# Weight-stationary projections: the high weights move over high and low activations in one 512-column matmul

## The chip, the cores and the metric

The kernel runs on one core of a Trainium2 chip. The metric is the device time of one execution in microseconds (us), the median of several runs; a shorter time is better. The engines of the core run side by side and wait for one another through semaphores: TensorE (PE for its matmuls, PEld for its loads of stationary operands), VectorE (DVE), ScalarE (ACT), GpSimd (POOL) and SyncE (SP), whose queue issues the weight transfers.

## The reference

Two layers, each of three sub-layers with an RMSNorm before and after, on 256 tokens of 1024 features, in float32. Layer 0 mixes tokens by a gated short convolution, layer 1 by a gated DeltaNet (GDN).

```python
def swiglu(x, w_gate_up, w_down):
    gate, up = jnp.split(x @ w_gate_up, 2, axis=-1)
    return (jax.nn.silu(gate) * up) @ w_down

def short_conv_mixer(x, w_in, conv_w, w_out):
    b, c, v = jnp.split(x @ w_in, 3, axis=-1)
    y = b * causal_depthwise_conv(c * v, conv_w)
    return y @ w_out
...
    for i in range(DEPTH):
        g = norm_g[i]
        ff = swiglu(rms_norm(h, g[0]), ffn_w_gate_up[i, 0], ffn_w_down[i, 0])
        h = h + 0.5 * rms_norm(ff, g[1])
        m_in = rms_norm(h, g[2])
...
        h = h + rms_norm(mix, g[3])
        ff = swiglu(rms_norm(h, g[4]), ffn_w_gate_up[i, 1], ffn_w_down[i, 1])
        h = h + 0.5 * rms_norm(ff, g[5])
```

The four FFNs have 2816 hidden features each, so a gate-and-up weight is 1024 x 5632 and a down weight 2816 x 1024.

## The kernel before, in words

Every float32 factor is split into a high and a low part of a faster matmul type (float32r). A product is then the sum of three: high by high, high activations by low weights, low activations by high weights.

**Weights.** A unit is 512 KB of weights, 128 partitions x 1024. `unit` (L102) loads it into one of 3 `raw` buffers by the SP queue, ACT writes its high part `whi` (L111), DVE the low part `wlo` = raw - `whi` (L113). There are 8 pairs of `whi` and `wlo` buffers. A slab of an input projection is four units: 1024 input rows (8 steps k of 128) by 512 output columns. So two slabs fit on the chip.

**Activations.** After the pre-norm, `pre_norm` (L160) transposes a token tile of 128 tokens on PE and writes the high and low part of the transposed activations, `xh` and `xl`, each 128 partitions x 2 token tiles x 8 k x 128 tokens.

**Input projections.** The first slabs of a sub-layer (two; one in the first) go one token tile after the other, with the activations stationary and 512 weight columns moving (`act_group`, L203, lines L214, L215, L218). All later slabs go by `stat_group` (L237): 128 weight columns are stationary, the 256 tokens of both tiles move, and per k there are three matmuls of 256 columns, L245 (`whi`, `xh`), L246 (`whi`, `xl`) and L247 (`wlo`, `xh`), each with its own load of the stationary operand. All 24 matmuls of a group add into one 256-column half of a PSUM bank. A slab of an FFN has four groups: gate and up of two blocks j of 128 hidden features. The pool `ps` has four banks (tile name `mm`), `ps_acc` the other four.

**Reading the groups.** In an FFN, per j: ACT takes silu of the gate half from PSUM (L335, `sg`), DVE multiplies it by the up half from PSUM (L337, `hf`), ACT and DVE write its high and low part (L338, L339; `hh`/`hl` or parts of `hb`). In the short convolution, ACT copies one half (L386) and DVE multiplies (L387); in its last two slabs DVE multiplies the gate `y` by a whole bank of two groups (L405). In the GDN a short convolution reads the groups directly (L517, L519).

**Output projections.** `out_proj` (L251) goes in chunks of one unit, the activations stationary, 512 weight columns moving (L263, L264, L265), with token tile 1 six chunks behind tile 0.

**Order.** The program is written as one stream of PE work; the framework's scheduler places every instruction in the queue of its engine, and each engine works through its queue in that order. Chains of the GDN are resumed by ticks between groups. All DMAs of weights are issued by SP as `raw` buffers come free.

Of the kernel before, what the change touches and what calls it, by code (L numbers as in the profile page):

```python
# [24 lines left out]
LAG = 6  # chunks by which token tile 1 follows tile 0 in an output projection  # L25
SPLIT = 1024  # columns per hi/lo split instruction
HEAD = 2  # slabs whose token tiles are projected one after the other at the start of a sub-layer
HEAD0 = 1  # the same for the first sub-layer
NW = 8  # hi/lo weight units on chip
NRAW = 3  # raw weight units on chip  # L30
NSMALL = 22  # 2 KB slots
NBIG = 8  # 4 KB slots
NROW = 3  # [128, 1024] work rows
KQ_WAIT = 3  # waits of the side chains, in ticks
# [3 lines left out]
ORD = "00111222"  # which mark of the norm chain each head unit is split after  # L38
GORD = "00012222"  # the same in the GDN
GSPLIT = 1024  # SPLIT of the GDN head  # L40
TPOS = 1  # output projection steps left when the next input is transposed
DEFER = 4  # k steps by which the low part of the activations lags
DEFER0 = 0  # the same in the first sub-layer
# [3 lines left out]
GUACT = 1  # decay operands built on ScalarE  # L47
# [3 lines left out]
def trunk_kernel(ctx: ExitStack, tc: tile.TileContext, x, norm_g, w_gu, w_dn, sc_in, sc_cw, sc_out,  # L51
# [144 lines left out]

    def new_xT():
        xh = sp.tile([P, NT, KD, P], F32R, name="xh", bufs=1)
        xl = sp.tile([P, NT, KD, P], F32R, name="xl", bufs=1)
        return xh, xl  # L200

# [1 line left out]
    def act_group(pt, w, t, xh, xl, defer=0):  # L203
        """Activations of token tile t stationary; all columns of the slab move."""
        per = KD // len(w)
        width = w[0][0].shape[-1] // per
        def part(k):
            c = slice((k % per) * width, (k % per + 1) * width)
            return w[k // per][0][:, c], w[k // per][1][:, c]

        for k in range(KD + defer):
            if k < KD:
                hi, lo = part(k)
                PE.matmul(pt, lhsT=xh[:, t, k, :], rhs=hi, start=(k == 0), stop=False)  # L214
                PE.matmul(pt, lhsT=xh[:, t, k, :], rhs=lo, start=False, stop=False)  # L215
            if k >= defer:
                j = k - defer
                PE.matmul(pt, lhsT=xl[:, t, j, :], rhs=part(j)[0], start=False, stop=(j == KD - 1))  # L218
                if j % 2:
                    tk.tick()  # L220

    def head_slabs(ws, xh, xl, evac, mid, defer=DEFER):
        """The first slabs, one token tile after the other (weights of all of them stay)."""
        late = None
        for t in range(NT):
            if t == 1:
                mid()
            for i, w in enumerate(ws):
                n = w[0][0].shape[-1] * len(w) // KD
                pt = ps.tile([P, n], F32, name="mm")  # L230
                act_group(pt, w, t, xh, xl, 0 if i else defer)
                if late is not None:
                    late()
                late = evac(t, i, pt)
        return late

    def stat_group(ptile, w, col, xh, xl):  # L237
        """Weights of 128 columns stationary; both token tiles move."""
# [11 lines left out]

    def out_proj(srcs, yh, yl, finish, last, lag=LAG):  # L251
        """yh/yl(c, t) -> [128 ch, 128 tok] operands; accumulates token-major [128, 1024]."""
# [39 lines left out]
    def ffn_proj(layer, ab, xh, xl, mid, head=HEAD):  # L292
# [31 lines left out]
        for s in range(head, NSLAB):  # L324
            alloc(s)
            w = load_slab(src[s])
            for j in range(2):
                pt = ps.tile([P, 512], F32, name="mm")
                stat_group(pt[:, 0:256], w, j * P, xh, xl)
                stat_group(pt[:, 256:512], w, 256 + j * P, xh, xl)  # L330
                if late is not None:
                    late()
                    late = None
                sg = sp.tile([P, 256], F32, name="sg")
                S.activation(sg, pt[:, 0:256], AF.Silu)  # L335
                hf = sp.tile([P, 256], F32, name="hf")
                V.tensor_tensor(hf, sg, pt[:, 256:512], ALU.mult)  # L337
                S.activation(hh[s][:, j, :], hf, AF.Copy)  # L338
                V.tensor_tensor(hl[s][:, j, :], hf, hh[s][:, j, :], ALU.subtract)  # L339
# [5 lines left out]
    def sc_proj(xh, xl, mid):  # L345
# [32 lines left out]
        for s in range(4):  # L378
            if s >= HEAD:
                w = load_slab(sc_in[s])  # L380
                for j in range(2):
                    pt = ps.tile([P, 512], F32, name="mm")
                    stat_group(pt[:, 0:256], w, j * P, xh, xl)
                    stat_group(pt[:, 256:512], w, 256 + j * P, xh, xl)
                    sg = sp.tile([P, 256], F32, name="sg")
                    S.activation(sg, pt[:, 0:256], AF.Copy)  # L386
                    V.tensor_tensor(cv[s][:, j, :], sg, pt[:, 256:512], ALU.mult)  # L387
# [6 lines left out]
        for s in range(2):  # L394
            w = load_slab(sc_in[4 + s])
            for i in range(2):
# [4 lines left out]
                pt = ps.tile([P, 2, T], F32, name="mm")  # L401
                for j in range(2):
                    stat_group(pt[:, j, :], w, (2 * i + j) * P, xh, xl)
                hf = sp.tile([P, 2, T], F32, name="yb")
                V.tensor_tensor(hf, y[2 * s + i], pt, ALU.mult)  # L405
# [4 lines left out]
    def gdn_proj(xh, xl, mid):  # L410
# [14 lines left out]
        # -- beta, log decay and their exponentials, both token tiles at once --  # L425
# [15 lines left out]
        def gates():  # L441
# [10 lines left out]
            # log1p(e) = 2 atanh(z), z = e / (2 + e) <= 1/3, by its series in z^2  # L452
# [55 lines left out]
        # -- keys and queries, channel-major: short conv, silu --  # L508
# [29 lines left out]
        def kq_chain():  # L538
            """Per pair of key heads: norms, scaled decayed k k^T and k q^T, diagonal blocks."""
# [56 lines left out]
        # -- unit lower triangular inverse: 32x32 blocks one per lane, then 64x64 on the tensor engine --  # L596
# [53 lines left out]
        # -- values: conv, silu, token-major, scaled by |k| --  # L650
# [18 lines left out]
        # -- delta rule of four value heads over the two token tiles --  # L669
# [87 lines left out]
        # -- gate, norm weight, channel-major operands of the output projection --  # L757
# [29 lines left out]
        # -- order of work: head columns [b a | k0 q0 k1], [q1 k2 q2 k3], then q3, k4, q4, ... --  # L787
# [106 lines left out]
def layout(x, norm_g, ffn_w_gate_up, ffn_w_down, sc_w_in, sc_conv_w, sc_w_out,  # L894
# [3 lines left out]
    def slabs(w, groups, width):  # L898
        """(1024, groups*n*width) -> [n, 4, 128, 2*groups*width]."""
# [5 lines left out]
    def cols(parts, n):  # L905
        """(1024, width) -> [n, 128, 8 / n * width]."""
        w = np.concatenate(parts, axis=1)
        return c(w.reshape(n, KD // n, P, w.shape[1]).transpose(0, 2, 1, 3).reshape(n, P, -1))
# [51 lines left out]
```

## Time and profile before

| What | Value |
|---|---|
| Time, median of 3 runs | 1155.92 us (1155.24 to 1156.04) |
| Span of the profiled execution | 1153.1 us |
| What the median has beyond that span | 2.8 us |
| PE busy | 1119.9 us (97%), 7584 matmul records |
| PEld busy | 1013.7 us (88%) |
| DVE busy | 691.3 us (60%) |
| ACT busy | 600.8 us (52%) |
| Groups L245, L246, L247 | 1512 matmuls each |
| Mean granted TensorE clock | 0.995 |

The profile is of one execution, which has a span from its first to its last instruction and no other time of its own. A matmul record lasts from issue to the modelled end of its drain, so records overlap and a busy PE says little; the distance from one start to the next (the pitch) tells what a matmul takes of the stream. A granted clock of 1.0 is 2.4 GHz, of 0.5 is 1.2 GHz.

### The profile page before, as it was taken

How to read it: one execution, taken by the hardware profiler on the slowest of the kernel's cores; microseconds unless marked ns; L12 is line 12 of the kernel's file. 1: busy time of each engine (PE TensorE's matmuls, PEld its weight loads, DVE VectorE, ACT ScalarE, POOL GpSimd, SP SyncE). 2: the span in 40 equal slices, each digit the busy share in tenths (PEclk: the TensorE clock that was granted, in tenths of full speed). 3: DMA queues.
4: the chain of work that ended last, by engine and by line, in shares of the span. 5: the costliest groups of instructions: out<-in, count | busy, mean ns of one | idle time of the engine just before them, and what ended most of it. 6: DMA issues, size and time to landing. Idle time of an engine off the chain costs nothing.

```text
span 1153.1 us, 18985 instructions
## 1 busy us (share of the span) xinstructions
PE 1119.9 (97%) x7584; PEld 1013.7 (88%) x7584; DVE 691.3 (60%) x981; ACT 600.8 (52%) x1027; POOL 80.3 (7%) x145
## 2 busy tenths in 40 slices
PE   6999999999999999999999999888999999999997
PEld 5999987899799998789998887877998877999986
DVE  5665535785765553565554478778865567655443
ACT  5654534544554443555443368875676546545432
POOL 1000000000200000010000012210310212000000
PEclk9999999999999999999999999999899999999999
DMA  7755555665576455566555653246424145655552
GB/s 260 225 195 198 167 177 177 216 198 171 183 219 201 165 198 167 166 218 202 194 172 167 195 173 110 92 134 195 147 92 156 47 135 167 219 193 171 194 164 74
DMA packets 55959, 198.78 MB, mean 172 GB/s; under 512 B 6720, under 2 KB 7232, under 8 KB 55872
## 3 DMA queue, kind: packets, MB, share of 16 engines
q1 hardware_dynamic: 55872, 197.58, 52.9%
q8 instruction: 59, 0.97, 0.3%
q14 instruction: 28, 0.23, 0.1%
HBM read 196.51 MB, written 1.05 MB: 171 GB/s over the span
## 4 chain that ended last, share of the span: by engine, by line
PE 79%; DVE 7%; ACT 6%; DMA 4%; issue 2%; POOL 2%; SPq 0%; DVEq 0%; POOLq 0%; ACTq 0%
PE mm L245 15%; PE mm L247 15%; PE mm L246 15%; PE acc L263 7%; PE acc L264 7%; PE acc L265 7%; PE mm L214 3%; PE mm L215 3%; PE mm L218 3%; DVE wlo L113 2%; DMA raw<-in_w_gu 2%; ACT whi L111 2%; ACT blk L585 1%; ACT junk L145 1%; DVE kq L519 1%
## 5 line engine op out<-in xcount | busy, mean ns | idle before, releaser
L113 DVE TENSOR_TENSOR wlo<-raw,whi 128x1024 fp32r<-128x1024 f32 (+2 forms) x362 | 436.4, 1218 | 338.1 <-ACT whi L111 336.6
L111 ACT ACTIVATE whi<-raw 128x1024 fp32r<-128x1024 f32 (+2 forms) x362 | 373.2, 1052 | 362.2 <-PE acc L265 103.7
L245 PE MATMUL mm<-xh,whi 128*128 128x256 f32 x1512 | 432.1, 286 | 2.0 <-DVE kq L519 2.0
L246 PE MATMUL mm<-xl,whi 128*128 128x256 f32 x1512 | 430.3, 285 | 0.0
L247 PE MATMUL mm<-xh,wlo 128*128 128x256 f32 x1512 | 429.9, 284 | 0.1
L245 PEld LDWEIGHTS mm<-xh,whi 128*128 128x128 f32 x1512 | 291.4, 193 | 3.1 <-DVE kq L519 2.4
L246 PEld LDWEIGHTS mm<-xl,whi 128*128 128x128 f32 x1512 | 291.7, 193 | 0.5 <-issue 0.2
L247 PEld LDWEIGHTS mm<-xh,wlo 128*128 128x128 f32 x1512 | 291.5, 193 | 0.7 <-DVE wlo L113 0.3
L263 PE MATMUL acc<-whi,hb 128*128 128x512 f32 x352 | 137.1, 389 | 0.0
L264 PE MATMUL acc<-wlo,hb 128*128 128x512 f32 x352 | 135.8, 386 | 0.2 <-DVE wlo L113 0.2
L265 PE MATMUL acc<-whi,hb 128*128 128x512 f32 x352 | 135.7, 386 | 0.0
L215 PE MATMUL mm<-wlo,xh 128*128 128x512 f32 (+1 forms) x240 | 95.1, 396 | 1.5 <-DVE wlo L113 1.4
L214 PE MATMUL mm<-whi,xh 128*128 128x512 f32 (+1 forms) x240 | 95.5, 399 | 0.8 <-ACT xh L173 0.6
L218 PE MATMUL mm<-whi,xl 128*128 128x512 f32 (+1 forms) x240 | 88.7, 392 | 0.0
L263 PEld LDWEIGHTS acc<-whi,hb 128*128 128x128 f32 x352 | 66.2, 188 | 14.1 <-issue 1.2
L264 PEld LDWEIGHTS acc<-wlo,hb 128*128 128x128 f32 x352 | 66.2, 188 | 13.5 <-DVE wlo L113 0.5
L265 PEld LDWEIGHTS acc<-whi,hb 128*128 128x128 f32 x352 | 66.1, 188 | 13.3
L151 POOL TENSOR_SCALAR rstd<-ss 128x1 f32<-128x1 f32 x24 | 12.2, 509 | 825.9 <-ACT junk L145 825.9
L215 PEld LDWEIGHTS mm<-wlo,xh 128*128 128x128 f32 x240 | 45.7, 190 | 12.6 <-DVE wlo L113 4.4
L214 PEld LDWEIGHTS mm<-whi,xh 128*128 128x128 f32 x240 | 45.7, 191 | 11.4 <-ACT xh L173 2.3
L218 PEld LDWEIGHTS mm<-whi,xl 128*128 128x128 f32 x240 | 45.6, 190 | 9.2 <-DVE xl L174 0.4
L335 ACT ACTIVATE sg<-mm 128x256 f32<-128x256 f32 x74 | 27.5, 372 | 33.8 <-PE mm L247 33.8
(202 smaller groups left out, 976.1 us busy)
## 6 DMA issues: line engine op xcount, KB each, us to landing
raw<-in_w_gu SPq DMA_DIRECT2D x176, 512.0 KB, 4.3
raw<-in_w_dn SPq DMA_DIRECT2D x88, 512.0 KB, 3.7
raw<-in_sc_in SPq DMA_DIRECT2D x24, 512.0 KB, 4.2
raw<-in_gdn_z SPq DMA_DIRECT2D x16, 512.0 KB, 3.8
raw<-in_gdn_v SPq DMA_DIRECT2D x16, 512.0 KB, 4.2
raw<-in_gdn_out SPq DMA_DIRECT2D x16, 512.0 KB, 3.3
gamma<-in_norm_g SPq DMA_DIRECT2D x12, 512.0 KB, 5.8
raw<-in_gdn_a SPq DMA_DIRECT2D x9, 512.0 KB, 4.2
```

The lines of the kernel that those rows point to most:

```text
L111: S.activation(hi[:, r], raw[:, r], AF.Copy)
L113: V.tensor_tensor(lo[:, r], raw[:, r], hi[:, r], ALU.subtract)
L214: PE.matmul(pt, lhsT=xh[:, t, k, :], rhs=hi, start=(k == 0), stop=False)
L215: PE.matmul(pt, lhsT=xh[:, t, k, :], rhs=lo, start=False, stop=False)
L218: PE.matmul(pt, lhsT=xl[:, t, j, :], rhs=part(j)[0], start=False, stop=(j == KD - 1))
L245: PE.matmul(ptile, lhsT=hi, rhs=xh[:, :, k, :], start=(k == 0), stop=False)
L246: PE.matmul(ptile, lhsT=hi, rhs=xl[:, :, k, :], start=False, stop=False)
L247: PE.matmul(ptile, lhsT=lo, rhs=xh[:, :, k, :], start=False, stop=(k == KD - 1))
L263: PE.matmul(o, lhsT=yh(c, t), rhs=hi[:, r], start=(c == 0), stop=False)
L264: PE.matmul(o, lhsT=yh(c, t), rhs=lo[:, r], start=False, stop=False)
L265: i = PE.matmul(o, lhsT=yl(c, t), rhs=hi[:, r], start=False, stop=(c == n - 1)).ins
L335: S.activation(sg, pt[:, 0:256], AF.Silu)
```

## The change

`xh` and `xl` become the two halves of one tile `x2`. A new `wide_group` takes the place of `stat_group` in the FFNs and in the short convolution (the GDN keeps `stat_group`). Per k it makes one matmul of 512 columns, `whi` stationary, over the 256 high and the 256 low activation columns, into both halves of a PSUM bank, and one of 256 columns, `wlo` by the high activations, into the second half. The first half then holds high by high, the second the two corrections. `total` reads a group: ACT copies the second half to `corr`, DVE adds the first half from PSUM to it. A group now fills a bank of its own, and silu and the products read the sums in SBUF. Comments are taken out as well, and line numbers move: L264 and L265 are the wide and the narrow matmul, L273 and L274 the copy and the add.

```diff
     def new_xT():
-        xh = sp.tile([P, NT, KD, P], F32R, name="xh", bufs=1)
-        xl = sp.tile([P, NT, KD, P], F32R, name="xl", bufs=1)
-        return xh, xl
...
+        x2 = sp.tile([P, 2, NT, KD, P], F32R, name="x2", bufs=1)
+        both.append(x2)
+        return x2[:, 0], x2[:, 1]
...
+    def wide_group(w, col):
...
+        pt = ps.tile([P, 2, T], F32, name="mm")
+        xx = both[-1]
...
+            PE.matmul(pt, lhsT=hi, rhs=xx[:, :, :, k, :], start=(k == 0), stop=False)
+            PE.matmul(pt[:, 1, :], lhsT=lo, rhs=xx[:, 0, :, k, :], start=False, stop=(k == KD - 1))
...
+    def total(pt, dst):
...
+        c = sp.tile([P, T], F32, name="corr")
+        S.activation(c, pt[:, 1, :], AF.Copy)
+        V.tensor_tensor(dst, pt[:, 0, :], c, ALU.add)
...
-                pt = ps.tile([P, 512], F32, name="mm")
-                stat_group(pt[:, 0:256], w, j * P, xh, xl)
-                stat_group(pt[:, 256:512], w, 256 + j * P, xh, xl)
+                pg = wide_group(w, j * P)
+                pu = wide_group(w, 256 + j * P)
...
-                sg = sp.tile([P, 256], F32, name="sg")
-                S.activation(sg, pt[:, 0:256], AF.Silu)
-                hf = sp.tile([P, 256], F32, name="hf")
-                V.tensor_tensor(hf, sg, pt[:, 256:512], ALU.mult)
+                sg = sp.tile([P, T], F32, name="sg")
+                total(pg, sg)
+                S.activation(sg, sg, AF.Silu)
+                hf = sp.tile([P, T], F32, name="hf")
+                total(pu, hf)
+                V.tensor_tensor(hf, sg, hf, ALU.mult)
...
-                    stat_group(pt[:, j, :], w, (2 * i + j) * P, xh, xl)
-                hf = sp.tile([P, 2, T], F32, name="yb")
-                V.tensor_tensor(hf, y[2 * s + i], pt, ALU.mult)
+                    total(wide_group(w, (2 * i + j) * P), hf[:, j, :])
+                V.tensor_tensor(hf, y[2 * s + i], hf, ALU.mult)
```

PE's queue inside a weight-stationary stream of the first FFN, before:

```order
L245 MATMUL mm<-xh,whi 128x256
L246 MATMUL mm<-xl,whi 128x256
L247 MATMUL mm<-xh,wlo 128x256
L245 MATMUL mm<-xh,whi 128x256
L246 MATMUL mm<-xl,whi 128x256
L247 MATMUL mm<-xh,wlo 128x256
```

and of the changed kernel (`x_90` is the tile `x2`):

```order
L264 MATMUL mm<-x_90,whi 128x512
L265 MATMUL mm<-x_90,wlo 128x256
L264 MATMUL mm<-x_90,whi 128x512
L265 MATMUL mm<-x_90,wlo 128x256
L264 MATMUL mm<-x_90,whi 128x512
L265 MATMUL mm<-x_90,wlo 128x256
```

Three matmuls and three loads of a k step have become two of each; the moving columns of a step are 768 in both.

DVE's queue over one slab in the middle of the first FFN, before:

```order
L113 TENSOR_TENSOR wlo<-raw,whi 128x1024 x2
L337 TENSOR_TENSOR hf<-sg,mm 128x256
L113 TENSOR_TENSOR wlo<-raw,whi 128x1024
L339 TENSOR_TENSOR hb<-hf,hb 128x256
L113 TENSOR_TENSOR wlo<-raw,whi 128x1024
L337 TENSOR_TENSOR hf<-sg,mm 128x256
L339 TENSOR_TENSOR hb<-hf,hb 128x256
```

and one slab there in the changed kernel:

```order
L113 TENSOR_TENSOR wlo<-raw,whi 128x1024 x2
L274 TENSOR_TENSOR hf<-mm,corr 128x256
L113 TENSOR_TENSOR wlo<-raw,whi 128x1024
L363 TENSOR_TENSOR hf<-sg,hf 128x256
L274 TENSOR_TENSOR sg<-mm,corr 128x256
L365 TENSOR_TENSOR hb<-hf,hb 128x256
L113 TENSOR_TENSOR wlo<-raw,whi 128x1024
L274 TENSOR_TENSOR hf<-mm,corr 128x256
L363 TENSOR_TENSOR hf<-sg,hf 128x256
L365 TENSOR_TENSOR hb<-hf,hb 128x256
L274 TENSOR_TENSOR sg<-mm,corr 128x256
```

Four adds L274, one per group, have come between the four splits L113 of the next units.

ACT's queue over one slab of the same FFN, before:

```order
L111 ACTIVATE whi<-raw 128x1024
L335 ACTIVATE sg<-mm 128x256
L338 ACTIVATE hb<-hf 128x256
L111 ACTIVATE whi<-raw 128x1024 x3
L335 ACTIVATE sg<-mm 128x256
L338 ACTIVATE hb<-hf 128x256
```

and in the changed kernel:

```order
L273 ACTIVATE corr<-mm 128x256
L111 ACTIVATE whi<-raw 128x1024
L360 ACTIVATE sg<-sg 128x256
L111 ACTIVATE whi<-raw 128x1024
L273 ACTIVATE corr<-mm 128x256
L111 ACTIVATE whi<-raw 128x1024
L273 ACTIVATE corr<-mm 128x256
L364 ACTIVATE hb<-hf 128x256
L111 ACTIVATE whi<-raw 128x1024
L360 ACTIVATE sg<-sg 128x256
L273 ACTIVATE corr<-mm 128x256
L364 ACTIVATE hb<-hf 128x256
```

Four copies L273 have come in, each waiting for the end of its group on PE, and the four `whi` splits of a slab stand between them.

## Rows read from the trace of the kernel before

**Rows 1.** The page's first part (busy time and share of the span by engine, instructions) and, from the view of the cores, the span and the mean granted clock.

```profile
PE 1119.9 (97%) x7584; PEld 1013.7 (88%) x7584; DVE 691.3 (60%) x981; ACT 600.8 (52%) x1027; POOL 80.3 (7%) x145
core 0: 1153.1 us, clock 0.995
```

**Rows 2.** Everything that PE waited for in the whole span, longest in total first: who waited for whom, us in total, times, longest us.

```profile
PE mm L171 <- DVE xs L164: 12.3, 6, 8.9
PE mm L662 <- ACT yb L506: 3.7, 1, 3.7
PE acc L551 <- ACT kq L506: 2.1, 1, 2.1
PE mm L245 <- DVE kq L519: 2.0, 1, 2.0
PE acc L554 <- DVE KQ L578: 1.7, 1, 1.7
PE mm L215 <- DVE wlo L113: 1.4, 2, 1.2
PE acc L637 <- ACT blk L630: 0.7, 1, 0.7
PE acc L467 <- DVE glog L463: 0.6, 1, 0.6
PE mm L214 <- ACT xh L173: 0.6, 1, 0.6
PE acc L551 <- ACT junk L563: 0.6, 2, 0.4
PE acc L264 <- DVE wlo L113: 0.2, 1, 0.2
PE acc L626 <- DVE blk L613: 0.2, 1, 0.2
```

**Rows 3.** Five stretches that lie inside the weight-stationary streams of the first FFN, the short convolution and the other three FFNs: the stretch in us, its length, busy us (and instructions) of PE, PEld, DVE, ACT and POOL, granted clock, share of the DMA engines, GB/s.

```profile
30.00:142.00 112.00, 112.00 (x934) 111.94 (x933) 63.68 (x81) 59.25 (x85) 0.00 (x0) 1.00 0.60 195
228.00:273.00 45.00, 45.00 (x378) 45.00 (x377) 33.39 (x51) 21.54 (x28) 0.00 (x0) 1.00 0.65 202
322.00:425.00 103.00, 103.00 (x861) 103.00 (x860) 56.89 (x75) 50.94 (x75) 0.00 (x0) 1.00 0.59 193
513.00:616.00 103.00, 103.00 (x861) 103.00 (x861) 57.02 (x75) 51.13 (x75) 0.00 (x0) 1.00 0.60 192
982.00:1085.00 103.00, 103.00 (x861) 103.00 (x860) 57.02 (x74) 50.84 (x75) 0.00 (x0) 1.00 0.58 191
```

**Rows 4.** The groups of the three matmuls of `stat_group`, from the page: out and in, shapes, count, then busy us, mean ns of one, and PE's idle time before them.

```profile
L245 PE MATMUL mm<-xh,whi 128*128 128x256 f32 x1512 | 432.1, 286 | 2.0 <-DVE kq L519 2.0
L246 PE MATMUL mm<-xl,whi 128*128 128x256 f32 x1512 | 430.3, 285 | 0.0
L247 PE MATMUL mm<-xh,wlo 128*128 128x256 f32 x1512 | 429.9, 284 | 0.1
```

**Rows 5.** PE in order of time inside the stream of the first FFN: start in us, length in us, instruction. The first two and the last of 52 rows in a run.

```profile
59.84 0.28 PE L245 MATMUL mm<-xh,whi 128*128 128x256 f32 x1
59.96 0.28 PE L246 MATMUL mm<-xl,whi 128*128 128x256 f32 x1
...
65.95 0.28 PE L245 MATMUL mm<-xh,whi 128*128 128x256 f32 x1
```

**Rows 6.** The same view in an output projection, 512 columns: the first two and the last of 19 rows in a run.

```profile
159.72 0.39 PE L265 MATMUL acc<-whi,hb 128*128 128x512 f32 x1
159.94 0.39 PE L263 MATMUL acc<-whi,hb 128*128 128x512 f32 x1
...
163.80 0.39 PE L265 MATMUL acc<-whi,hb 128*128 128x512 f32 x1
```

**Rows 7.** The same view at the end of the last output projection, where the moving operand is 256 columns that lie side by side: the first and the last of 28 rows in a run.

```profile
1142.73 0.28 PE L264 MATMUL acc<-wlo,hh 128*128 128x256 f32 x1
...
1145.97 0.28 PE L264 MATMUL mm<-wlo,hh 128*128 128x256 f32 x1
```

**Rows 8.** Groups with their shapes kept apart: splits of a unit, and the readers of a group in the FFNs; columns as in rows 4.

```profile
L113 DVE TENSOR_TENSOR wlo<-raw,whi 128x1024 fp32r<-128x1024 f32 x356 | 431.2, 1223 | 335.8 <-ACT whi L111 334.4 <-PE mm L246 0.5
L111 ACT ACTIVATE whi<-raw 128x1024 fp32r<-128x1024 f32 x356 | 368.5, 1056 | 355.7 <-PE acc L265 102.0 <-DMA raw<-in_w_gu 83.7 <-PE mm L246 71.5
L337 DVE TENSOR_TENSOR hf<-sg,mm 128x256 f32<-128x256 f32 x74 | 30.9, 417 | 14.8 <-ACT sg L335 14.4
L335 ACT ACTIVATE sg<-mm 128x256 f32<-128x256 f32 x74 | 27.5, 372 | 33.8 <-PE mm L247 33.8
L339 DVE TENSOR_TENSOR hb<-hf,hb 128x256 fp32r<-128x256 f32 x50 | 21.1, 422 | 12.1 <-ACT hb L338 12.1
L338 ACT ACTIVATE hb<-hf 128x256 fp32r<-128x256 f32 x50 | 20.9, 418 | 30.0 <-DVE hf L337 30.0
```

**Rows 9.** Transfers of gate-and-up units, from the page: count, size, median us from issue to landing.

```profile
raw<-in_w_gu SPq DMA_DIRECT2D x176, 512.0 KB, 4.3
```

**Rows 10.** PE in order of time in the GDN, columns as in rows 5: the end of a wait, and narrow matmuls behind it.

```profile
806.94 1.11 PE L662 MATMUL mm<-ident,yb 128*128 128x128 f32 x4 [3.69 <-ACT yb L506]
...
808.07 0.41 PE L246 MATMUL mm<-xl,whi 128*128 128x256 f32 x1
...
809.99 0.38 PE L246 MATMUL mm<-xl,whi 128*128 128x256 f32 x1
```

More of the change, by code (lines that the diff above doesn't have):

```diff
@@ L195, in post_norm @@
         return sq, st
+    both = []
     def new_xT():
-        xh = sp.tile([P, NT, KD, P], F32R, name="xh", bufs=1)
-        xl = sp.tile([P, NT, KD, P], F32R, name="xl", bufs=1)
-        return xh, xl
+        x2 = sp.tile([P, 2, NT, KD, P], F32R, name="x2", bufs=1)
+        both.append(x2)
+        return x2[:, 0], x2[:, 1]
     def act_group(pt, w, t, xh, xl, defer=0):
@@ L249, in stat_group @@
                 tk.tick()
+    def wide_group(w, col):
+        pt = ps.tile([P, 2, T], F32, name="mm")
+        xx = both[-1]
+        per = KD // len(w)
+        width = w[0][0].shape[-1] // per
+        for k in range(KD):
+            c = (k % per) * width + col
+            hi = w[k // per][0][:, c:c + P]
+            lo = w[k // per][1][:, c:c + P]
+            PE.matmul(pt, lhsT=hi, rhs=xx[:, :, :, k, :], start=(k == 0), stop=False)
+            PE.matmul(pt[:, 1, :], lhsT=lo, rhs=xx[:, 0, :, k, :], start=False, stop=(k == KD - 1))
+            if k % 4 == 3:
+                tk.tick()
+        return pt
+    def total(pt, dst):
+        c = sp.tile([P, T], F32, name="corr")
+        S.activation(c, pt[:, 1, :], AF.Copy)
+        V.tensor_tensor(dst, pt[:, 0, :], c, ALU.add)
     def out_proj(srcs, yh, yl, finish, last, lag=LAG):
@@ L381, in sc_proj @@
                 for j in range(2):
[L382 to L387, printed above, removed]
+                    pc = wide_group(w, j * P)
+                    pv = wide_group(w, 256 + j * P)
+                    sg = sp.tile([P, T], F32, name="sg")
+                    total(pc, sg)
+                    hf = sp.tile([P, T], F32, name="hf")
+                    total(pv, hf)
+                    V.tensor_tensor(cv[s][:, j, :], sg, hf, ALU.mult)
                     if late is not None:
@@ L400, in sc_proj @@
                 hl.append(b)
-                pt = ps.tile([P, 2, T], F32, name="mm")
+                hf = sp.tile([P, 2, T], F32, name="yb")
                 for j in range(2):
-                    stat_group(pt[:, j, :], w, (2 * i + j) * P, xh, xl)
-                hf = sp.tile([P, 2, T], F32, name="yb")
-                V.tensor_tensor(hf, y[2 * s + i], pt, ALU.mult)
+                    total(wide_group(w, (2 * i + j) * P), hf[:, j, :])
+                V.tensor_tensor(hf, y[2 * s + i], hf, ALU.mult)
                 S.activation(a, hf, AF.Copy)
```

## Prediction

> **What bounds the kernel now.** I began with the busy shares and the clock: PE is busy for 97% of the span, DVE for 60%, ACT for 52%, and the granted clock is 0.995 [rows 1]. A busy PE alone says little, so I went on to what PE waited for. The list for the whole span sums to 26 us, 12.3 of it at the norms' transposes (L171); of the three matmuls of `stat_group` only one wait shows, 2.0 us behind DVE L519, which is in the GDN [rows 2]. Then the stretches inside the five weight-stationary streams that change: PE and its loads are busy all the time, the clock is 1.00, and DVE is busy 55 to 57% in the FFNs and 74% in the short convolution (33.39 of 45.00) [rows 3]. So in these streams the pitch of PE's instructions sets the time, and everything else has room.
>
> The pitch comes from the order in time. Narrow matmuls: from 59.84 to 65.95 there are 51 steps, 6.11 / 51 = 119.8 ns [rows 5], and the longer sample of rows 7 gives 3.24 / 27 = 120.0 ns. Wide ones: from 159.72 to 163.80 there are 18 steps, 226.7 ns [rows 6]. At the full 2.4 GHz, 256 columns take 106.7 ns and 512 take 213.3 ns. Both pitches are 13.3 ns longer. The extra is therefore a price per matmul, with its load, and not per column. The runs of the moving operand don't matter either: in rows 5 it is two runs of 128 columns (one for each token tile), in rows 7 one run of 256, and the pitch is the same. In the change the wide operand is four runs of 128.
>
> **The change part by part.**
>
> *PE.* The groups are 1512 / 8 = 189 [rows 4]. Of these the GDN keeps 9 for keys and queries and 16 for values. The others are 10 slabs of four in the first FFN and 9 slabs in each of the other three, 37 x 4 = 148, and 16 in the short convolution: 164 groups, 1312 steps k. A step now takes 3 x 120.0 = 360.0 ns and will take 226.7 + 120.0 = 346.7 ns. The sum is 1312 x 13.3 ns = 17.5 us; a group takes 8 x 346.7 ns = 2.77 us in place of 2.88.
>
> *DVE and ACT.* Each group adds a copy on ACT and an add on DVE. Neither shows in this shape before; the nearest rows are L335 (ACT from PSUM, 372 ns) and L337 (DVE, one operand from PSUM, 417 ns) [rows 8], and I take these. Silu and the product stay, with operands in SBUF, 418 and 422 ns by L338 and L339. A slab of an FFN then asks of DVE 4 x 1.223 + 4 x 0.417 + 4 x 0.422 = 8.25 us, and of ACT 4 x 1.056 + 4 x 0.372 + 4 x 0.418 = 7.38 us, while PE takes 32 x 346.7 ns = 11.09 us. The extra 164 x 0.42 = 69 us of DVE and 61 us of ACT are hidden beside PE as long as nothing that PE waits for is late. Their price is zero under that cover; without it, at most their own length, which is much more than the gain. So what follows is on waits, since these engines work in the order of their queues.
>
> *Banks.* A group now holds a whole bank of four, so a group waits for the add of the fourth group before it. That leaves three groups, 8.3 us, between the end of one and the need for its bank. In ACT's queue a copy has at most one `whi` between it and the copy before; in the worst place it stands behind a `whi` and a silu. Take that: one split 1.06, silu 0.42, copy 0.37, and on DVE a split 1.22, a product 0.42 and the add 0.42, 3.9 us. Even with the 4.3 us of a transfer in front [rows 9] it is 8.2 us, and the transfers are issued a slab ahead. I take no wait.
>
> *Units.* The buffers hold two slabs, so the units of slab s+2 are split while s+1 runs. The first `whi` can start when the last group of slab s is 0.7 us old. The fourth stands behind the first two copies of slab s+1 in ACT's queue: about 3.6 us into that slab, or, when its transfer is late, 4.5; its `wlo` is done at about 7 of 11.1 us. It is needed 2.1 us into slab s+2, 6 us later. The output projection's first units come the same way; only those after the last copy of the stream come later than before, by the copy, the add and the product, 1.2 us, and they are needed 8 us after the stream.
>
> *The short convolution* is the narrow place, for DVE also has the convolution there: 33.4 us and 16 x 0.417 = 6.7 give 40.1 of the 45.0 - 1.7 = 43.3 us that the stretch will last, 93%. By the queue its splits come 2 to 3 us before PE needs them. I take zero, with 6.7 us (all of the adds in the open) as the other end.
>
> *The rest.* Transposes, head slabs and output projections keep their instructions, and so does the GDN, where a narrow matmul reads the same runs of `x2`. The GDN's waits can fall differently against the clock: behind a wait of 3.69 us narrow matmuls ran at 1.92 / 9 = 213 ns [rows 10], which is 256 columns at 1.2 GHz. All of the clock that is missing in the span is 0.5% of 1153.1 us, 5.8 us, so I give this 4 us either way and zero in the sum.
>
> Sum: the span goes from 1153.1 to 1135.6 us. The median of the runs lies 2.8 us above that span; with the same distance the time is 1138.4 us.
>
> **The rivals.**
>
> *The load sets the pitch.* PEld is busy without a break in the streams [rows 3], so a third fewer loads could be worth more than 13 ns: the step falls to its columns alone, 768 / 2.4 = 320 ns, 40 ns less, 52 us in all, 1103 us. Against it: a wide matmul has twice the time to hide its load and still pays the same 13.3 ns. Chance 2%. Perfetto Trace Analysis (the Trainium skill), section "Identifying the Most-Contended Engine", takes the busy share of LDWEIGHTS as the measure of TensorE's headroom, and by it this rival would be likely; the trace speaks against that reading here, since records of loads overlap as those of matmuls do.
>
> *The extra goes with the columns, so nothing is saved.* Then the wide matmul costs two narrow ones, 240 ns, and the time stays at 1155.9. Against it stand rows 6 with 226.7, though with another operand. If a fifth of the extra, 2.7 ns, is fixed, the gain is 1312 x 2.7 ns = 3.5 us and the time 1152.4. Chance 4%, a quarter of it for such a fixed part. TensorE: Matmul & The Clock Gate (the Trainium skill), section "Back-to-back issue gap", gives an isolated stream's pitch as the columns over 2.4 GHz plus about 2.5 ns per matmul; by that figure a merged pair saves an estimated 3.3 us in all. The trace does not agree: its pitches are 13.3 ns above the columns' time [rows 5 to 7], with a load for each matmul.
>
> *Part of it is given back.* DVE is late in the short convolution (up to 6.7 us) and at the turn of sub-layers (five streams, about 0.4 us each): 1138.4 + 8.7 = 1147. For it: the 93%. Against it: the slack by the queue. Chance 6%.
>
> *The other side: a wait in every slab.* Each slab's first groups wait for a bank or a unit, because the copies that wait for PE now stand in front of the `whi` splits. It decides at 17.5 / 41 slabs = 0.43 us a slab (37 of the FFNs, 4 of the short convolution). With a wait of 1 us a slab the time is 1138.4 + 41 = 1179 us. For it: four more waits on PE in ACT's queue per slab, and half the banks per group. Against it: the 6 us of slack. Chance 6%.
>
> **How the numbers follow.** The forecast, 1138.4, has 82%, with a range of its own of 1134.4 to 1142.4 for the GDN's clock and small waits. With the partial case the range is 1134.4 to 1147. A measurement of this kernel tells 0.2% (2.3 us) from no change. Faster: the forecast, the partial case, the cheaper load and a quarter of the columns' case, 82 + 6 + 2 + 1 = 91%. Same: the rest of the columns' case, 3%. Slower: the wait in every slab, 6%.
>
> **What would show it.** Right: inside the streams the starts alternate by 227 and 120 ns; the first FFN's stream of 40 groups (320 steps) falls by 320 x 13.3 ns = 4.3 us and each later FFN's by 3.8; the new lines show no idle time of PE; DVE's total rises to about 760 us, ACT's to about 665. Wrong: wide starts at 240 ns or at 200; a wait of a wide matmul on DVE's add (the bank) or on L113; idle time of PE at the first output chunks of the short convolution.

## The result and the profile after

The changed kernel takes 1146.45 us (median of 4 runs, 1144.5 to 1148.82), the kernel before 1155.66 us (4 runs, 1155.24 to 1156.04). The ratio is 0.9925 with a 95% interval of 0.9908 to 0.9942, so it is 9.2 us faster. Forecast were 1138.4 us, 17.5 us less than the kernel before; a little over half of that came. The profiled execution took 1144.5 us with a span of 1142.8.

Busy time by engine, from the page of the changed kernel, and its span and clock from the view of the cores; they answer to [rows 1].

```profile
PE 1108.3 (97%) x6272; PEld 942.5 (82%) x6272; DVE 759.1 (66%) x1145; ACT 652.4 (57%) x1187; POOL 80.3 (7%) x145
core 0: 1142.8 us, clock 0.994
```

PE has 1312 instructions fewer, one for each step. DVE and ACT are busy for 67.8 and 51.6 us more.

Five stretches inside the streams that changed (columns as in [rows 3]):

```profile
30.00:135.00 105.00, 105.00 (x608) 91.87 (x607) 77.01 (x118) 68.41 (x120) 0.00 (x0) 1.00 0.64 208
228.00:268.00 40.00, 40.00 (x229) 34.68 (x228) 33.73 (x60) 19.76 (x30) 0.00 (x0) 1.00 0.62 195
318.00:416.00 98.00, 98.00 (x557) 85.05 (x557) 70.47 (x107) 60.25 (x107) 0.00 (x0) 1.00 0.60 196
508.00:605.00 97.00, 97.00 (x552) 84.10 (x551) 69.16 (x106) 59.09 (x105) 0.00 (x0) 1.00 0.61 200
975.00:1073.00 98.00, 98.00 (x557) 84.99 (x556) 70.36 (x107) 60.12 (x107) 0.00 (x0) 1.00 0.60 198
```

PE is still busy without a break at the full clock. DVE now has 71 to 73% in the FFNs and 84% in the short convolution.

The longest waits of PE over the whole span (columns as in [rows 2]), and from the page the two new matmuls and the copy (columns as in [rows 4]):

```profile
PE mm L171 <- DVE xs L164: 12.1, 6, 8.7
PE mm L688 <- ACT yb L532: 3.8, 1, 3.8
PE acc L577 <- ACT kq L532: 3.6, 2, 3.1
PE mm L247 <- DVE kq L545: 2.0, 1, 2.0
PE acc L580 <- DVE KQ L604: 1.7, 1, 1.7
PE mm L217 <- DVE wlo L113: 1.4, 2, 1.2
...
```

```profile
L264 PE MATMUL mm<-x,whi 128*128 128x512 f32 x1312 | 462.7, 398 | 0.0
L265 PE MATMUL mm<-x,wlo 128*128 128x256 f32 x1312 | 367.3, 280 | 0.0
...
L273 ACT ACTIVATE corr<-mm 128x256 f32<-128x256 f32 x164 | 62.0, 379 | 85.9 <-PE mm L265 85.9
```

The waits are those of before, but for L577, which waits 3.6 us in the GDN where the same instruction waited 2.1. The six rows left out are of 0.6 us or less, and none is of L264 or L265: no wait shows at the new lines. The split by shape gives the add L274:

```profile
L274 DVE TENSOR_TENSOR sg<-mm,corr 128x256 f32<-128x256 f32 x78 | 32.9, 422 | 29.9 <-ACT corr L273 29.4
L274 DVE TENSOR_TENSOR hf<-mm,corr 128x256 f32<-128x256 f32 x78 | 32.7, 419 | 5.1 <-ACT corr L273 4.2
```

So the missing 8 us are in no list of waits. They are in the pitch. PE in order of time (start, length, instruction), first in the first FFN:

```profile
59.92 0.39 PE L264 MATMUL mm<-x,whi 128*128 128x512 f32 x1
60.15 0.27 PE L265 MATMUL mm<-x,wlo 128*128 128x256 f32 x1
60.27 0.40 PE L264 MATMUL mm<-x,whi 128*128 128x512 f32 x1
...
62.00 0.39 PE L264 MATMUL mm<-x,whi 128*128 128x512 f32 x1
```

then in the second FFN:

```profile
400.12 0.40 PE L264 MATMUL mm<-x,whi 128*128 128x512 f32 x1
400.36 0.28 PE L265 MATMUL mm<-x,wlo 128*128 128x256 f32 x1
400.48 0.40 PE L264 MATMUL mm<-x,whi 128*128 128x512 f32 x1
400.71 0.28 PE L265 MATMUL mm<-x,wlo 128*128 128x256 f32 x1
400.83 0.40 PE L264 MATMUL mm<-x,whi 128*128 128x512 f32 x1
401.06 0.28 PE L265 MATMUL mm<-x,wlo 128*128 128x256 f32 x1
401.18 0.40 PE L264 MATMUL mm<-x,whi 128*128 128x512 f32 x1
...
402.24 0.40 PE L264 MATMUL mm<-x,whi 128*128 128x512 f32 x1
```

Six steps take 62.00 - 59.92 = 2.08 us, 346.7 ns each, in the first FFN, and 402.24 - 400.12 = 2.12 us, 353.3 ns, in the second. In the second the steps come in threes of 360, 350 and 350 ns, 401.18 - 400.12 = 1.06 us. Taken over whole slabs the mean step is 346.67 ns in the first FFN and 353.3 in the short convolution and the three later FFNs; before it was 360.00 in all five.

The length of a stream shows in the first and the last of its starts. In the second FFN, and with the end of the third FFN's and the start of the fourth's, before:

```profile
322.00 0.36 PE L245 MATMUL mm<-xh,whi 128*128 128x256 f32 x1
...
425.84 0.28 PE L247 MATMUL mm<-xh,wlo 128*128 128x256 f32 x1
...
616.59 0.28 PE L247 MATMUL mm<-xh,wlo 128*128 128x256 f32 x1
...
981.55 0.36 PE L245 MATMUL mm<-xh,whi 128*128 128x256 f32 x1
```

and after:

```profile
316.80 0.48 PE L264 MATMUL mm<-x,whi 128*128 128x512 f32 x1
...
418.74 0.28 PE L265 MATMUL mm<-x,wlo 128*128 128x256 f32 x1
...
606.92 0.28 PE L265 MATMUL mm<-x,wlo 128*128 128x256 f32 x1
...
973.19 0.48 PE L264 MATMUL mm<-x,whi 128*128 128x512 f32 x1
```

The second FFN's stream takes 101.94 us in place of 103.84, 1.9 less, and so do the third's and fourth's. The first loses 4.5 (111.19 for 115.69), the short convolution 0.85 (45.40 for 46.25), together 11.1 us. The stretch between the third and fourth FFN's streams, with the GDN in it, took 366.3 us in place of 365.0. The span is 10.3 us shorter.

### The profile page after: what moved, and what is told of

The parts are those of the page before. It is cut to its first block, busy times and chain, and to the rows that moved or that the text cites. A ratio compares the mean times of both kernels' runs of the same rounds, so it can differ in the third digit from the quotient of the medians.

```text
span 1142.8 us, 16740 instructions
## 1 busy us (share of the span) xinstructions
PE 1108.3 (97%) x6272; PEld 942.5 (82%) x6272; DVE 759.1 (66%) x1145; ACT 652.4 (57%) x1187; POOL 80.3 (7%) x145
## 4 chain that ended last, share of the span: by engine, by line
PE 81%; DVE 6%; ACT 5%; DMA 3%; issue 2%; POOL 2%; SPq 0%; DVEq 0%; POOLq 0%; ACTq 0%
PE mm L264 27%; PE mm L265 14%; PE acc L288 7%; PE acc L289 7%; PE acc L290 7%; PE mm L216 3%; PE mm L217 3%; PE mm L220 3%; DVE wlo L113 2%; ACT whi L111 1%; DMA raw<-in_gdn_v 1%; ACT blk L611 1%; PE mm L247 1%; DVE kq L545 1%; ACT junk L145 1%
## 5 line engine op out<-in xcount | busy, mean ns | idle before, releaser
L113 DVE TENSOR_TENSOR wlo<-raw,whi 128x1024 fp32r<-128x1024 f32 (+2 forms) x362 | 440.0, 1220 | 234.0 <-ACT whi L111 231.6
L264 PE MATMUL mm<-x,whi 128*128 128x512 f32 x1312 | 462.7, 398 | 0.0
L265 PE MATMUL mm<-x,wlo 128*128 128x256 f32 x1312 | 367.3, 280 | 0.0
L264 PEld LDWEIGHTS mm<-x,whi 128*128 128x128 f32 x1312 | 246.4, 188 | 60.0
L265 PEld LDWEIGHTS mm<-x,wlo 128*128 128x128 f32 x1312 | 247.5, 189 | 0.1
L273 ACT ACTIVATE corr<-mm 128x256 f32<-128x256 f32 x164 | 62.0, 379 | 85.9 <-PE mm L265 85.9
L217 PE MATMUL mm<-wlo,x 128*128 128x512 f32 (+1 forms) x240 | 94.9, 395 | 1.5 <-DVE wlo L113 1.4
L216 PE MATMUL mm<-whi,x 128*128 128x512 f32 (+1 forms) x240 | 95.3, 398 | 0.7 <-ACT x L173 0.6
L220 PE MATMUL mm<-whi,x 128*128 128x512 f32 (+1 forms) x240 | 88.6, 392 | 0.0
L247 PE MATMUL mm<-x,whi 128*128 128x256 f32 x200 | 60.0, 300 | 2.0 <-DVE kq L545 2.0
L248 PE MATMUL mm<-x,whi 128*128 128x256 f32 x200 | 58.8, 294 | 0.0
L249 PE MATMUL mm<-x,wlo 128*128 128x256 f32 x200 | 58.5, 292 | 0.0
L217 PEld LDWEIGHTS mm<-wlo,x 128*128 128x128 f32 x240 | 45.7, 190 | 12.2 <-DVE wlo L113 3.8
L216 PEld LDWEIGHTS mm<-whi,x 128*128 128x128 f32 x240 | 45.6, 190 | 11.0 <-ACT x L173 2.3
```

What stands on the lines that cost most here:

```text
L113: V.tensor_tensor(lo[:, r], raw[:, r], hi[:, r], ALU.subtract)
L247: PE.matmul(ptile, lhsT=hi, rhs=xh[:, :, k, :], start=(k == 0), stop=False)
L264: PE.matmul(pt, lhsT=hi, rhs=xx[:, :, :, k, :], start=(k == 0), stop=False)
L265: PE.matmul(pt[:, 1, :], lhsT=lo, rhs=xx[:, 0, :, k, :], start=False, stop=(k == KD - 1))
L273: S.activation(c, pt[:, 1, :], AF.Copy)
```

## The experiments

Three theories for the lost 6.6 ns a step, by the names that the expectations use:

- *Rhythm*: wide and narrow matmuls that alternate have a steady rhythm of their own, and each turn (a change from narrow to wide and back) can cost something that a uniform stream doesn't show. Nothing outside PE is needed for it.
- *Contention*: the new copies and adds, which read PSUM while PE writes there, slow PE's stream.
- *Four runs*: the wide operand is four runs of 128 columns, and reading it costs more than the wide matmuls of [rows 6] showed.

All diffs are against the changed kernel, `part(k)` gives the pair of `whi` and `wlo` of step k, and the table at the end has the mean step in each stream. Each kernel has one profile, the changed one three and the order of two and two two.

**The same kernel again.** No edit.

> The changed kernel once more, to see whether a stream keeps its rhythm from run to run. In the first profile a step of a wide and a narrow matmul took 346.7 ns in the first FFN's stream and 353.3 ns in the other four. Rhythm theory (alternating widths settle into one of a few steady rhythms where a stream starts, by the phase in which it starts): other runs have other streams at other rhythms, 346.7, 353.3 and perhaps 360 ns, each the same from the start of a stream to its end; times between 1138 and 1150 us. Contention theory (the added copies and adds read the banks and slow PE): the rhythm is the same in the same stream in every run, about 1146 us. Four-runs theory (the wide operand is four runs of 128 columns, which costs up to 7 ns): 353 ns in every stream, also in the first.

Measured: 1145.55 us (5 runs, 1143.71 to 1150.86), ratio 0.9913 [0.9899, 0.9928]. In its profile the first FFN too has 353.3 ns:

```profile
59.63 0.40 PE L264 MATMUL mm<-x,whi 128*128 128x512 f32 x1
...
61.75 0.40 PE L264 MATMUL mm<-x,whi 128*128 128x512 f32 x1
```

Six steps in 2.12 us, by the same code in the same place as above. The stream has two steady rhythms, and code, addresses and operand layout don't choose between them.

This trace holds both of them in one stream. In its first slab, behind the second group, PE makes two transposes (L341) for the slab ahead of the stream:

```profile
29.42 0.39 PE L264 MATMUL mm<-x,whi 128*128 128x512 f32 x1
...
31.50 0.39 PE L264 MATMUL mm<-x,whi 128*128 128x512 f32 x1
...
31.85 0.38 PE L341 MATMUL mm<-ident,hf 128*128 128x128 f32 x2
...
33.13 0.40 PE L264 MATMUL mm<-x,whi 128*128 128x512 f32 x1
...
35.25 0.40 PE L264 MATMUL mm<-x,whi 128*128 128x512 f32 x1
```

Six steps take 2.08 us ahead of the transposes and 2.12 us behind them. So a stream can change its rhythm where it is interrupted, and it keeps what it has behind the transposes to its end.

**Eight wide, then eight narrow.** In a group all wide matmuls come first; the same 16 matmuls and the same readers.

```diff
-            PE.matmul(pt, lhsT=hi, rhs=xx[:, :, :, k, :], start=(k == 0), stop=False)
-            PE.matmul(pt[:, 1, :], lhsT=lo, rhs=xx[:, 0, :, k, :], start=False, stop=(k == KD - 1))
+            PE.matmul(pt, lhsT=part(k)[0], rhs=xx[:, :, :, k, :], start=(k == 0), stop=False)
+        for k in range(KD):
+            PE.matmul(pt[:, 1, :], lhsT=part(k)[1], rhs=xx[:, 0, :, k, :], start=False, stop=(k == KD - 1))
```

> In each group first the eight wide matmuls, then the eight narrow ones; the same instructions in another order. Rhythm theory: the widths change twice a group and not sixteen times, wide steps take 226.7 ns and narrow ones 120.0, a group about 2.78 us; time 1138 to 1139.5 us, and runs lie as close as those of the kernel before (1 us). Contention and four-runs theory: nothing of the loss goes, 1145 to 1147 us; by the four-runs theory the wide steps take 233 ns.

Measured: 1142.11 us (4 runs, 1140.02 to 1142.58), ratio 0.9881 [0.9867, 0.9896]. The order alone gains, which contention and four runs don't give, but less than the rhythm theory said (1138 to 1139.5 us): a step takes 349.17 ns in every stream, a group 2.793 us and not 2.773.

```profile
400.36 2.00 PE L265 MATMUL mm<-x,whi 128*128 128x512 f32 x8
402.20 1.11 PE L267 MATMUL mm<-x,wlo 128*128 128x256 f32 x8
403.15 2.00 PE L265 MATMUL mm<-x,whi 128*128 128x512 f32 x8
```

Behind the turn the wide starts lie 234, 236, 228 and 232 ns apart and then settle at 226 to 231; narrow ones have 113 at the turn and then 120. A turn costs 8 x (349.17 - 346.67) = 20 ns.

**Three narrow, with the new banks and readers.** PE's work is again that of before, three matmuls of 256 columns a step; banks, copies and adds stay as changed.

```diff
-            PE.matmul(pt, lhsT=hi, rhs=xx[:, :, :, k, :], start=(k == 0), stop=False)
+            PE.matmul(pt[:, 0, :], lhsT=part(k)[0], rhs=xx[:, 0, :, k, :], start=(k == 0), stop=(k == KD - 1))
+        for k in range(KD):
+            PE.matmul(pt[:, 1, :], lhsT=part(k)[0], rhs=xx[:, 1, :, k, :], start=(k == 0), stop=False)
```

> One part alone: three narrow matmuls per step as in the kernel before, but a bank per group and the copy and add of the changed kernel. Rhythm theory: 120.0 ns a matmul, no wait, the time of the kernel before within 0.2% (1153.5 to 1158). Contention theory: the added copies and adds slow PE as they did in the change, 1312 steps by 5 to 7 ns more, 1162 to 1165 us.

Measured: 1155.19 us (10 runs, 1151.56 to 1157.68), ratio 0.9998 [0.9987, 1.0009].

```profile
400.62 1.12 PE L265 MATMUL mm<-x,whi 128*128 128x256 f32 x8
...
406.38 1.12 PE L265 MATMUL mm<-x,whi 128*128 128x256 f32 x8
```

Two groups take 5.76 us, 16 steps of 360.0 ns, to the hundredth what they took before. With all copies and adds in place a uniform stream loses nothing: contention is refuted for uniform streams, and the new work of DVE and ACT is shown to be hidden.

**Corrections not read.** Silu and the products read the first half from PSUM again; the matmuls stay.

```diff
-                total(pg, sg)
-                S.activation(sg, sg, AF.Silu)
+                S.activation(sg, pg[:, 0, :], AF.Silu)
...
-                total(pu, hf)
-                V.tensor_tensor(hf, sg, hf, ALU.mult)
+                V.tensor_tensor(hf, sg, pu[:, 0, :], ALU.mult)
```

> The changed kernel's PE stream, but ACT and DVE read only the first half of each bank, by as many instructions as in the kernel before: the two correction products are computed and not added. Rhythm theory: steps of 346.7, 353.3 or 360 ns by stream as in the changed kernel, 1138 to 1150 us, mean about 1146. Contention theory: 346.7 ns in every stream, 1138 us.

Measured: 1146.58 us (4 runs, 1144.5 to 1147.74), ratio 0.9922 [0.9906, 0.9937]; its profile has the span of the changed kernel's, 1142.8 us, with 346.66 ns in the first FFN and 353.3 in the others. DVE's 71 us less of work change nothing. So the mixture is as slow without the added reads: contention falls here too.

**All wide.** Both matmuls of a step take 512 columns, so the stream is uniform, with four runs of 128 in every operand. The sum then holds the product of the two low parts as well.

```diff
-            PE.matmul(pt[:, 1, :], lhsT=lo, rhs=xx[:, 0, :, k, :], start=False, stop=(k == KD - 1))
+            PE.matmul(pt, lhsT=part(k)[1], rhs=xx[:, :, :, k, :], start=False, stop=(k == KD - 1))
```

> The low weights move over high and low activations too, so that all matmuls of these streams have 512 columns; the product low by low is added to the second half's neighbour, which the reference has in its full float32 product. No turn of width is left. Price of a turn: 2 x 226.7 = 453.3 ns a step in every stream, so 1312 x 93.3 ns = 122 us over the kernel before, about 1277 us. Four-runs theory: 233 ns a matmul, 466 ns a step, 1294 us.

Measured: 1277.18 us (one run).

```profile
400.17 0.39 PE L265 MATMUL mm<-x,whi 128*128 128x512 f32 x1
...
404.25 0.39 PE L265 MATMUL mm<-x,whi 128*128 128x512 f32 x1
```

Nine steps in 4.08 us, 453.3 ns, which is 2 x 226.7: the pitch of [rows 6] holds for this operand too, in all five streams. The four-runs theory falls. What is left is the mixture of widths.

**Two wide, two narrow** (run twice, the second time timed beside the changed kernel). Steps go in pairs.

```diff
-        for k in range(KD):
...
+        for k in range(0, KD, 2):
+            for q in (k, k + 1):
+                PE.matmul(pt, lhsT=part(q)[0], rhs=xx[:, :, :, q, :], start=(q == 0), stop=False)
+            for q in (k, k + 1):
+                PE.matmul(pt[:, 1, :], lhsT=part(q)[1], rhs=xx[:, 0, :, q, :], start=False, stop=(q == KD - 1))
```

> Two wide, then two narrow matmuls, four turns of width in a group where the changed kernel has eight and the order of eight and eight has one. A turn from narrow to wide and back costs 6.7 ns (353.3 - 346.7) in the usual rhythm of the changed kernel and 19.6 ns a group in the order of eight and eight. If a turn has a fixed price of 6.7 ns: 350.0 ns a step. If a turn after more than one narrow matmul costs 20 ns: 356.7. If only single neighbours cost: 346.7.

> Two wide, two narrow once more, timed against the kernel before. A step took 348.33 ns in all five streams and should again, 1312 x 11.67 ns = 15.3 us less PE time than the kernel before; the rest of the program as before: 1139 to 1141.5 us, ratio 0.986 to 0.988. If the earlier 1137.75 us was the order's and not the GDN's luck: below 1139.

Measured: 1137.75 us the first time (one run); then 1139.13 us (4 runs, 1138.57 to 1141.65), ratio to before 0.9863 [0.9848, 0.9879].

```profile
399.98 0.63 PE L266 MATMUL mm<-x,whi 128*128 128x512 f32 x2
400.44 0.40 PE L268 MATMUL mm<-x,wlo 128*128 128x256 f32 x2
400.67 0.63 PE L266 MATMUL mm<-x,whi 128*128 128x512 f32 x2
...
408.34 0.63 PE L266 MATMUL mm<-x,whi 128*128 128x512 f32 x2
```

24 steps in 8.36 us, 348.3 ns, the same in all ten streams of the two profiles: 2 x (348.33 - 346.67) = 3.3 ns a turn, and no second rhythm. None of the three values that were expected came, so the price of a turn is neither fixed nor nothing.

**The changed kernel beside it.** No edit, on the same chip.

> The changed kernel on the same chip as the order of two and two, with a third profile. Streams two to five: 353.3 ns again, as in all profiles of this order. First stream: 346.7 or 353.3 ns; if it depends on how its first units arrive, either can come. 1144 to 1147 us, 4 to 7 us over the order of two and two.

Measured: 1146.83 us (5 runs, 1146.76 to 1147.06), ratio 0.9926 [0.9913, 0.994]; 346.66 ns in the first FFN and 353.3 in the rest. So the paired order is faster than both kernels, by 7.7 us than the changed one, where 4 to 7 were expected, and by 16.7 than before. Of the 8.2 us between the two spans the streams give 4.8 (462.9 and 458.1 us). The others lie in stretches whose instructions are the same in both kernels: 1.9 in the one with the GDN, 1.3 between the short convolution's stream and the second FFN's (49.35 and 48.06 us), 0.6 ahead of the first stream, less 0.4 elsewhere. All profiles together have 363.7 to 368.2 us with the GDN and 48.0 to 49.5 us behind the short convolution, so only the 4.8 us are shown to come from the order.

**Mirrored steps.** Every second step has its narrow matmul first, so that two narrow and two wide ones lie side by side without moving work between steps.

```diff
+            for half in ((0, 1) if k % 2 == 0 else (1, 0)):
+                if half == 0:
+                    PE.matmul(pt, lhsT=part(k)[0], rhs=xx[:, :, :, k, :], start=(k == 0), stop=(k == KD - 1))
+                else:
+                    PE.matmul(pt[:, 1, :], lhsT=part(k)[1], rhs=xx[:, 0, :, k, :], start=False, stop=False)
```

> Wide, narrow, narrow, wide and so on: also four turns a group, but the second step of each two begins with the narrow matmul. Fixed price of a turn: 350.0 ns a step. Price of the longer run: 356.7. No price: 346.7. By the four-runs theory 353.3, as in every order.

Measured: 1141.43 us (one run), 348.33 ns in all streams, the rhythm of the pairs and again none of the values expected. So the rhythm goes with the widths that stand side by side, not with the step that a matmul belongs to. Its time is 2 to 4 us longer than theirs, though its streams are 0.3 to 0.4 us shorter; its stretch with the GDN took 367.2 us against their 363.7 and 364.4, at a granted clock of 0.993 against 0.996 in the whole span. The instructions of that stretch are the same in all three.

**The last step swapped.** The mirrored loop with `(0, 1) if k < KD - 1 else (1, 0)`: one break of the alternation a group.

> The changed kernel's order, but in the last step of each group the narrow matmul goes first: once a group two narrow ones and, across the border, two wide ones stand together. If the rhythm is set anew by every break, streams show 346.7 and 353.3 ns by turns, a mean between; if the rhythm of 353.3 belongs to alternation itself and the first stream's 346.7 is the exception, all streams stay near 353.

Measured: 1148.1 us (one run), 352.5 ns in every stream. A break in the order in each group does not bring the alternation into its cheaper rhythm. The first FFN doesn't have it here either; by one profile, and with a stream that changes from run to run anyway, this can't be put down to the swap.

**Longer runs.** Four wide and four narrow (the loop of the pairs with 4 in place of 2), and sixteen and sixteen over two groups, whose two banks are then filled together:

```diff
-    def wide_group(w, col):
...
+    def wide_pair(w, cols):
+        pts = [ps.tile([P, 2, T], F32, name="mm") for _ in cols]
...
+        for pt, col in zip(pts, cols):
+            for k in range(KD):
+                PE.matmul(pt, lhsT=part(k, col, 0), rhs=xx[:, :, :, k, :], start=(k == 0), stop=False)
+        for pt, col in zip(pts, cols):
+            for k in range(KD):
+                PE.matmul(pt[:, 1, :], lhsT=part(k, col, 1), rhs=xx[:, 0, :, k, :], start=False, stop=(k == KD - 1))
```

> Four wide, four narrow: two turns a group. A turn cost 0 or 6.7 ns after one matmul of a width, 3.3 after two, 20 after eight. If the price grows from two on with the length of the run: between 3.3 and 20 a turn, a step of 347.5 to 351.7 ns. If it is 20 as soon as the run is longer than two: 351.7.

> Sixteen wide matmuls over two groups and two banks, then sixteen narrow ones. If the price of a turn has an end at 20 ns: 346.67 + 20 / 16 = 347.9 ns a step in all streams. If it goes on growing with the run: 349.2, as with eight. Both groups of a pair now end together and give back their banks later: a wait for a bank would show at the first wide matmul.

Measured: 1142.72 us and 1142.56 us (one run each). Fours have 350.0 to 350.8 ns, worse than pairs and than eights: a turn costs 4 x 3.3 to 4.2 = 13 to 17 ns, between the pairs' 3.3 and the eights' 20, and is paid twice as often as with eights. Sixteens have 347.9 ns in the FFNs, 16 x 1.25 = 20 ns again, so from two matmuls in a row to eight the price of a turn grows, and then no more. In the short convolution they take 364.4. Two new rows stand in PE's list of waits, the first in the first slab of the first FFN (which the means below leave out), the second in the short convolution:

```profile
PE mm L265 <- DVE hb L347: 1.2, 1, 1.2
...
PE mm L265 <- DVE yb L277: 0.9, 1, 0.9
```

Both are a wide matmul behind DVE; the second, behind the adds L277, is what the prediction named for the case that banks don't come free. Two banks at a time were one too many there.

All streams side by side, mean step in ns over whole slabs behind the first, and the five streams' sum from their first start to their last:

| Kernel | FFN 1 | short conv | FFN 2 | FFN 3 | FFN 4 | streams, us |
|---|---|---|---|---|---|---|
| before; three narrow | 360.00 | 360.00 | 360.00 | 360.00 | 360.00 | 473.5 (before) |
| changed | 346.67 | 353.28 | 353.3 | 353.3 | 353.3 | 462.4 |
| changed, again | 353.32 | 353.28 | 353.3 | 353.35 | 353.3 | 464.6 |
| corrections not read | 346.66 | 353.28 | 353.35 | 353.3 | 353.3 | 462.6 |
| last step swapped | 352.5 | 352.5 | 352.5 | 352.5 | 352.5 | 462.8 |
| two and two | 348.33 | 348.33 | 348.33 | 348.33 | 348.33 | 458.0, 458.1 |
| mirrored | 348.33 | 348.33 | 348.33 | 348.33 | 348.33 | 457.7 |
| four and four | 350.83 | 350.84 | 350.0 | 350.0 | 350.0 | 460.7 |
| eight and eight | 349.17 | 349.17 | 349.17 | 349.17 | 349.17 | 459.1 |
| sixteen and sixteen | 347.91 | 364.36 | 347.92 | 347.92 | 347.89 | 460.2 |

## Why the prediction was right, and where it was not

**Direction and stated range held, the forecast's own range did not.** Faster, at 1146.45 within 1134.4 to 1147, near its upper end, but outside the 1134.4 to 1142.4 that the forecast gave itself. No rival came true. The load alone doesn't set the pitch (no stream's mean step came under 346.7); the extra doesn't go with the columns (453.3 ns for two wide matmuls and not 480); no slab waits. The time lies where "Part of it is given back" put it, 1147, but by another way: the waits of that rival are nowhere in the list. That the stated range covers the result is luck; it was widened for waits that did not come, and what was lost is of the pitch.

**The term that was mis-sized is the step of "PE": "will take 226.7 + 120.0 = 346.7 ns".** Each pitch is right for a uniform stream, by [rows 5 to 7] and by the kernels with three narrow and with two wide matmuls. Their sum was taken for a mixture that no row of before showed, and the forecast's own range left no room for another. It held in the first FFN's stream, though even there as a sum alone (the starts lie 230 to 233 and 112 to 118 ns apart, not 227 and 120); in the other four (992 of the 1312 steps) a step took 353.3 ns, so a step saved 6.7 ns and not 13.3. That is 992 x 6.67 = 6.6 us, which takes 17.5 down to 10.9, and the five streams gave 11.1; their first slabs make the rest. By streams: 4.5 us in the first FFN for 4.3 forecast, 1.9 in each later FFN for 3.8, 0.85 in the short convolution for 128 x 13.3 ns = 1.7. The sign that the prediction named for a wrong step, wide starts at 240, was nearly it: in these four streams wide matmuls took 232 to 241 ns, while narrow ones took 113 to 120.

**"DVE and ACT": right in place and size.** The add took 420 ns for 417, the copy 379 for 372, the totals 759.1 and 652.4 us for 760 and 665. ACT's groups sum to 706.9 us after 637.9, 69 more, and yet its busy time has grown by 51.6 only, since records that overlap count once there. That they are hidden is shown by the runs with three narrow matmuls and without the reads of the corrections.

**"Banks", "Units", "The short convolution": right.** No wait was added. DVE's 33.73 of 40.00 us in the middle of the short convolution is 84%, below the 93% taken for the whole stretch. That the room there has an end showed only when a kernel took two banks at once.

**"The rest": right in size.** The stretch with the GDN took 363.7 to 368.2 us in the profiles of these kernels, which leave its work alone, within the 4 us either way; in the changed kernel's profile 1.3 us more than before. From the streams' 11.1 us, less this and some tenths of other stretches, come the 10.3 of the spans. The medians differ by 9.2; the runs of the changed kernel alone lie 4.3 us apart.

**Loads and headroom.** PEld is busy for 91.87 / 105 = 87% of the first FFN's stretch, where it was 100% [rows 3]; a third of the loads went and the step lost 3.7% at most. Perfetto Trace Analysis (the Trainium skill), section "Identifying the Most-Contended Engine", has the busy share of LDWEIGHTS, beside the share of peak FLOPs, tell TensorE's headroom. For the share of loads these runs don't agree: it fell by an eighth while the step came closer to its columns' time (768 columns at 2.4 GHz are 320 ns). Records of loads overlap (192 ns each at a pitch of 120 in the kernel before), so their share says little here. TensorE: Matmul & The Clock Gate (the Trainium skill), section "Back-to-back issue gap", says that the spacing in a stream is set by the load and the matmul together; a price that depends on the neighbours' widths is compatible with that, but no run here shows the load's part in it.

**What stays open.** Why a turn costs what it does inside TensorE. In all kernels here a narrow matmul writes half a bank and a wide one a whole bank, so width and destination change together, and no run parts them. Open is also what decides in the first FFN between 346.7 and 353.3 ns. Three of four profiles of the alternating order had the cheap rhythm there and one had not. The time at which the stream starts alone doesn't decide: 25.93 us in the profile with 353.3 ns, 25.95 in one with 346.7. What the traces do show is where it is decided. No stream changes its rhythm behind the transposes L341 in its first slab. At them it goes from 346.7 to 353.3 ns in the changed kernel run again, and from 353.3 to 346.7 in the kernel that doesn't read the corrections. In the first FFN a late unit can interrupt the first slab too: in the third profile of the changed kernel the steps are those of the slower rhythm ahead of a wait of 0.3 us behind L113, and those of the faster one behind it. In the sixteen later streams no wait shows, and all have 353.3 ns on both sides of the transposes. That the moment of the interruption picks the rhythm fits this, but was not tried.

## What to carry to other kernels

A pitch read from a uniform stream is not a price to add up for a mixture; in these runs the sum was the least that a mixture took, and only three streams reached it. Where a change makes wide and narrow matmuls alternate, bound the step from above as well, and try the order of the matmuls as a variable of its own. Here pairs of each width cost 3.3 ns a turn, single ones mostly 6.7, and long runs 20; reordering within a group, which moves no work, took 7.7 us off 1146.8, of which 4.8 are shown to be the streams'. And when a forecast gain is missing while no list of waits has grown, measure the start-to-start distance in each stream separately, since one mean over the kernel would have hidden that one stream behaved as forecast and four did not.

## What was not expected of the hardware

A stream of the same instructions, at the full granted clock and without a wait, has more than one steady rhythm: 346.7 or 353.3 ns for a wide and a narrow matmul, each kept from the last interruption in the stream's first slab to its end. Runs of four show two as well, 350.0 and 350.8 ns by stream. The price of a turn depends on how long the runs are: 0 or 6.7 ns in alternation, 3.3 with two, 13 to 17 with four, 20 with eight and sixteen. Uniform streams keep their pitch beside the copies and adds that read PSUM: 120.0 ns for narrow matmuls with and without them, 226.7 for wide ones with them.
